# Gate stage of a two-layer hybrid attention network: gate chunks in pairs by seven block products, worked through branch by branch

## Chip, cores and metric

The kernel runs on one core of one Trainium2 chip. The metric is the device time of one launch in microseconds (us). The core's engines are PE (matmul, with a weight-load queue of its own), DVE (vector), ACT (scalar), POOL and SP; SP here only issues DMAs.

## The reference

Input `x` has 512 tokens of width 1024. Two layers; each is a feed-forward part, a token mix, and a second feed-forward part, each with a layer norm. The change lies in the token mix, after its three attentions have made `o_a`, `o_b`, `o_c` (512 tokens x 512 each):

```python
g = jax.nn.sigmoid(h @ w_gate + b_gate).reshape(B, S, N_BRANCH, D)
merged = g[:, :, 0] * (o_a @ w_br_a) + g[:, :, 1] * (o_b @ w_br_b) + g[:, :, 2] * (o_c @ w_br_c)
return merged @ w_out
```

`w_gate` is 1024 x 3072 (three branches of 1024), each `w_br` 512 x 1024, `w_out` 1024 x 1024. All in float32.

## The kernel before

Everything is held transposed: features on the 128 partitions, the 512 tokens along the row. A float32 value is split into a rounded part (`hi`, copied by ACT) and the rest (`lo`, a subtraction on DVE), and a product is three matmuls: hi x hi, hi x lo, lo x hi (`mm3`, lines 182 to 184, in the profile the names `xh`, `xl` for the token side and `hi`, `lo` for the weights). Raw weights come by DMA into a ring of three buffers (`wraw`), and are split into a pair of buffers (`unit`).

A *gate chunk* is 128 of the 3072 gate columns: 8 blocks of 128 rows, so 24 matmuls of 512 columns into one PSUM bank named `gate`, then a tanh on ACT (`gate_ev`, line 1462; the sigmoid is made from it). A *branch chunk* is 128 of 1024 columns of `w_br`: 4 blocks, 12 matmuls into a bank named `brp`. Let (br, d) be chunk d (0 to 7) of branch br (0 to 2). A layer has 24 gate chunks and 24 branch chunks. The gate chunks (0..2, 0) and the matmuls of (0, 1) and (1, 1) are done earlier, as filling between the attention's matmuls (there the bank is called `pj`); the other 19 gate chunks and all branch chunks make up the gate stage.

Before the change the stage goes chunk by chunk: for each d the gates of the three branches, then one item with the branch chunks of branches 1 and 2, and one with that of branch 0. Each item has a load (DMA and split), a matmul part and an evacuation, and loads run three items ahead:

```python
        for i in range(4, len(items)):
            items[i][1]()
            if i + ahead < len(items):
                items[i + ahead][0]()
            items[i][2]()
```

The evacuation multiplies (tanh + 1) with the branch product (line 1593), adds the three branches (1597) and splits the merged chunk into `mh`, `ml` (1599, 1600). The attention outputs of all three branches are split before the stage (1615, 1616). From the fifth item on, PE, POOL, ACT and DVE take their instructions in the written order (`in_order`); SP's order is a scheduler's. After the stage the merged sum is multiplied with `w_out` into eight banks (`acc`, lines 195 to 197), in the same order of four blocks first.

Both feed-forward parts already work in pairs of column chunks by seven block products of 256 columns instead of eight (`strassen`, line 647): four sums of weights (`Pair.sums`, 525 to 528), four sums of tokens made once (`token_sums`), and a few additions on the results (663 to 674). `sums_step` paces, on POOL, a copy of one element and one DMA that prepares weight sums for the next feed-forward part.

Of the kernel before, what the change touches and what calls it, by code (L numbers as in the profile page):

```python
# [13 lines left out]
OP = mybir.AluOpType  # L14
# [50 lines left out]
def body(tc, a, out, depth=DEPTH):  # L65
# [3 lines left out]
    def pool(name, bufs=1, side=None, **kw):  # L69
        return tc.alloc_tile_pool(name=name, bufs=bufs, side=side, **kw)  # L70
# [85 lines left out]
    def wsplit(raw, n=KD, step=None):  # L156
        hi, lo = unit()
        step = step or n
        for i in range(0, n, step):
            c = slice(i, i + step)  # L160
            nc.scalar.activation(hi[:, c], raw[:, c], AF.Copy)  # L161
            nc.vector.tensor_tensor(lo[:, c], raw[:, c], hi[:, c].bitcast(F32), op=OP.subtract)  # L162
# [677 lines left out]
    def mix(l, wts, pend, done_ffn, xap, xa, nxt):  # L840
# [11 lines left out]
        more_close()  # L852

        op = pool("op", side="right", reuse_waits="tile")
        o_t = [[op.tile([P, S], F32, name=f"o{br}{i}") for i in range(4)] for br in range(3)]
# [605 lines left out]
        def gate_ev(t, p, br, d):  # L1461
            nc.scalar.activation(t, p, AF.Tanh, scale=0.5, bias=bg[:, br, d:d + 1])
# [23 lines left out]
        def step(cur, prev, n):  # L1486


            for u in cur:
                while not need(u):  # L1490
                    pump(1)
                    n -= 1
            it, iu = chain(u.tr() for u in prev), chain(u.s() for u in cur)
            nt, ns = sum(u.ngrp for u in prev), sum(u.nseg for u in cur)
            pair = 2
            nt = (nt + pair - 1) // pair
            both = 2 if ns == 2 else 1
# [24 lines left out]
            for _ in it:  # L1522
                pass
            pump(last)
            if prev:
                po = ps("po", "po", (P, 4, P))
                for j, u in enumerate(prev):
                    u.pv(po[:, j])
                while narrow:
                    narrow.popleft()()  # L1530
                for j, u in enumerate(prev):
                    nc.scalar.activation(o_t[u.br][u.m][:, u.qb * P:(u.qb + 1) * P], po[:, j], AF.Copy)
# [8 lines left out]
        at.release()  # L1541
        more_open()
        tp_ = pool("tl", reuse_waits="tile")
        mh = tp_.tile([P, KD, S], F32R, name="mh")
        ml = tp_.tile([P, KD, S], F32R, name="ml")
        ohp = pool("ohp", reuse_waits="tile")
        oh = [[None] * 4 for _ in range(3)]
        ol = [[None] * 4 for _ in range(3)]
        for br in (1, 2, 0):
            for i in range(4):  # L1550
                oh[br][i] = ohp.tile([P, S], F32R, name=f"oh{br}{i}")
                ol[br][i] = ohp.tile([P, S], F32R, name=f"ol{br}{i}")
        def wbr(d, brs):
            r = wraw()
            for j, br in enumerate(brs):
                nc.sync.dma_start(r[:, 4 * j:4 * j + 4],
                                  wb[br].rearrange("(k p) f -> p k f", p=P)[:, :, d * P:(d + 1) * P])
            return wsplit(r[:, 0:4 * len(brs)], 4 * len(brs))

        def gate_item(d, br, bank=None):  # L1560
            st = K()

            def load():
                st.w = wcols(a["w_gate"][l], br * D + d * P)

            def go():
                st.p = ps(bank, "gate")
                proj(st.p, st.w)

            def ev():  # L1570
                t = g_t[d][br] = tp_.tile([P, S], F32, name="t", tag="t", bufs=4)
                gate_ev(t, st.p, br, d)
                sums_step(t)

            return load, go, ev

        def branch_item(d, brs):
            st = K()

            def load():  # L1580
                st.w = wbr(d, brs)

            def go():
                st.p = [ps(name="brp") for _ in brs]
                for j, br in enumerate(brs):
                    for k in range(4):
                        mm3(st.p[j], st.w, 4 * j + k, oh[br][k], ol[br][k], k == 0, k == 3)

            def ev():
                g = g_t[d]  # L1590
                for br, p in zip(brs, st.p):
                    t = g[br]
                    nc.vector.scalar_tensor_tensor(t, t, 1.0, p, op0=OP.add, op1=OP.mult)
                    if br != 2:
                        sums_step(t)
                    if br != 1:
                        nc.vector.tensor_tensor(g[1], g[1], t, op=OP.add)
                if brs[-1] == 0:
                    nc.scalar.activation(mh[:, d], g[1], AF.Copy)
                    nc.vector.tensor_tensor(ml[:, d], g[1], mh[:, d].bitcast(F32), op=OP.subtract)  # L1600

            return load, go, ev

        g_t = [gates0] + [[None] * 3 for _ in range(1, KD)]
        for br in range(2):
            t = g_t[1][br] = tp_.tile([P, S], F32, name="t", tag="t", bufs=4)
            gate_ev(t, held[br], br, 1)
        items = []
        for d in range(KD):
            items += [gate_item(d, br) for br in range(3) if d > 1] + [branch_item(d, brs) for brs in ((1, 2), (0,))]  # L1610
        for f in gate_item(1, 2, "sc"):
            f()
        for br in (1, 2, 0):
            for i in range(4):
                nc.scalar.activation(oh[br][i], o_t[br][i], AF.Copy)
                nc.vector.tensor_tensor(ol[br][i], o_t[br][i], oh[br][i].bitcast(F32), op=OP.subtract)
        ahead = 3
        for i, (load, go, ev) in enumerate(items[:4]):
            load()
            if i == 3:  # L1620
                for load, _, _ in items[4:4 + ahead]:
                    load()
            go()
            ev()
        order = in_order()
# [6 lines left out]
        ohp.release()  # L1632
        op.release()
        xap2, xa2 = alloc_xa()
        ro = pool("ro", side="right", reuse_waits="tile")
# [177 lines left out]
```

## Time and profile before

| | |
|---|---|
| median of 3 runs | 2431.03 us (2430.78 to 2431.32) |
| span of the profiled execution, first to last instruction | 2430.1 us |
| PE busy | 2417.4 us (99%) |
| DVE, ACT, POOL busy | 1837.6, 1192.0, 490.3 us |
| gate stage of layer 0, of layer 1 (us from the span's start) | 667 to 836, 1868 to 2036 |
| granted PE clock | 1.00 throughout |

The profile of one execution gives each engine's instructions with their line, names (written from read), shapes and duration, and the engine or DMA that ended the idle time before them. Matmuls are pipelined: the duration printed of one is longer than the distance to the next, and it is the distance that counts. "x12" marks merged instructions of one kind.

### The profile page before, as it was taken

Reading aid. Unit: us, or ns where it says so; the run is one execution under the profiler, and the core shown is the slowest. Engines: PE = TensorE matmul, PEld = TensorE weight load, DVE = VectorE, ACT = ScalarE, POOL = GpSimd, SP = SyncE. Lnnn points to the kernel's source line nnn. Section 1 sums busy time; section 2 is a strip of 40 time slices with the busy share of each in tenths; the row PEclk is TensorE's granted clock in tenths of the full one; section 3 lists DMA queues with packets and bytes.
Section 4 is the critical chain, followed back from the end, with each engine's and each line's share of the span. In section 5 each row is a group of like instructions: output and inputs, shape, how many; then the busy total and the mean of one; then the engine's idle time right before and its main releaser. Section 6 shows DMA issues by size and latency. Waiting matters only on the chain.

```text
span 2430.1 us, 40766 instructions
## 1 busy us (share of the span) xinstructions
PE 2417.4 (99%) x15448; PEld 2141.6 (88%) x15448; DVE 1837.6 (76%) x3614; ACT 1192.0 (49%) x2304; POOL 490.3 (20%) x684
## 2 busy tenths in 40 slices
PE   9999999999999999999999999999999999999998
PEld 8999887888888899998899998878888888999987
DVE  6899985687654369999879999666776434799997
ACT  4444644577642234445544456455766222344463
POOL 4232402144410001124000004022443100000040
PEclk9999999999999999999999999999999999999999
DMA  7888754676493436887533347546764833333373
GB/s 207 225 224 216 256 159 132 174 166 153 107 254 97 128 105 162 210 209 238 187 109 105 105 129 252 151 139 166 165 141 112 247 104 109 105 99 106 107 241 121
DMA packets 422581, 390.01 MB, mean 160 GB/s; under 512 B 20473, under 2 KB 352393, under 8 KB 422385
## 3 DMA queue, kind: packets, MB, share of 16 engines
q1 hardware_dynamic: 385792, 287.00, 39.8%
q0 software_dynamic: 36592, 100.41, 17.3%
q8 instruction: 122, 2.00, 0.3%
q14 instruction: 75, 0.61, 0.1%
HBM read 360.02 MB, written 93.38 MB: 187 GB/s over the span
## 4 chain that ended last, share of the span: by engine, by line
PE 98%; DMA 1%; issue 0%; ACT 0%; DVE 0%; SPq 0%; DVEq 0%; POOLq 0%; POOL 0%; ACTq 0%
PE acc L331 18%; PE pg L647 17%; PE pu L647 9%; PE pj L182 6%; PE pj L184 6%; PE pj L183 6%; PE pv L647 4%; PE gate L182 3%; PE gate L183 3%; PE gate L184 3%; PE brp L183 2%; PE brp L182 2%; PE brp L184 2%; PE sN L1258 2%; PE ptN L1300 1%; PE po L1319 1%
## 5 line engine op out<-in xcount | busy, mean ns | idle before, releaser
L162 DVE TENSOR_TENSOR lo<-raw,hi 128x1024 fp32r<-128x1024 f32 (+2 forms) x262 | 301.7, 1165 | 248.8 <-ACT hi L161 248.2
L161 ACT ACTIVATE hi<-raw 128x1024 fp32r<-128x1024 f32 (+2 forms) x262 | 258.0, 1003 | 195.2 <-PE acc L331 52.9
L182 PE MATMUL pj<-xh,hi 128*128 128x512 f32 (+1 forms) x720 | 267.0, 371 | 1.0 <-ACT hi L161 1.0
L184 PE MATMUL pj<-xh,lo 128*128 128x512 f32 (+1 forms) x720 | 254.7, 354 | 0.5 <-DVE lo L162 0.5
L183 PE MATMUL pj<-xl,hi 128*128 128x512 f32 (+1 forms) x720 | 254.4, 353 | 0.1
L647 PE MATMUL pg<-xh,lo 128*128 128x256 f32 x864 | 244.5, 283 | 0.0
L647 PE MATMUL pg<-xl,hi 128*128 128x256 f32 x864 | 244.5, 283 | 0.0
L647 PE MATMUL pg<-xh,hi 128*128 128x256 f32 x864 | 244.5, 283 | 0.0
L331 PE MATMUL acc<-hi,sh 128*128 128x512 f32 x568 | 221.5, 390 | 0.0
L331 PE MATMUL acc<-lo,sh 128*128 128x512 f32 x568 | 221.0, 389 | 0.0
L331 PE MATMUL acc<-hi,sl 128*128 128x512 f32 x568 | 221.0, 389 | 0.0
L352 POOL COPY pace<-sh 64x1 f32<-64x1 f32 x16 | 94.5, 5909 | 479.8 <-ACT sh L592 479.8
L544 DVE TENSOR_TENSOR lo<-ws,hi 128x1024 fp32r<-128x1024 f32 x144 | 175.2, 1217 | 0.0
L647 PEld LDWEIGHTS pg<-xl,hi 128*128 128x128 f32 x864 | 165.9, 192 | 0.2
L647 PEld LDWEIGHTS pg<-xh,hi 128*128 128x128 f32 x864 | 165.9, 192 | 0.2
L647 PEld LDWEIGHTS pg<-xh,lo 128*128 128x128 f32 x864 | 165.9, 192 | 0.0
L647 PE MATMUL pu<-th,hi 128*128 128x256 f32 x576 | 163.0, 283 | 0.0
L647 PE MATMUL pu<-tl,hi 128*128 128x256 f32 x576 | 163.0, 283 | 0.0
L647 PE MATMUL pu<-th,lo 128*128 128x256 f32 x576 | 163.0, 283 | 0.0
L184 PEld LDWEIGHTS pj<-xh,lo 128*128 128x128 f32 x720 | 136.1, 189 | 20.4 <-DVE lo L162 0.8
L541 ACT ACTIVATE hi<-ws 128x1024 fp32r<-128x1024 f32 x144 | 143.9, 1048 | 16.9 <-DVE ws L526 15.3
L182 PEld LDWEIGHTS pj<-xh,hi 128*128 128x128 f32 x720 | 136.4, 189 | 16.7 <-issue 3.7
(374 smaller groups left out, 6645.9 us busy)
## 6 DMA issues: line engine op xcount, KB each, us to landing
raw<-in_ffn_w_dram SPq DMA_DIRECT2D x228, 512.0 KB, 4.5
ts<-in_ffn_w_dram POOLq DMA_DIRECT2D x72, 768.0 KB, 7.5
raw<-in_w_in_dram SPq DMA_DIRECT2D x56, 512.0 KB, 4.1
raw<-ts SPq DMA_DIRECT2D x52, 512.0 KB, 4.2
raw<-in_w_gate_dram SPq DMA_DIRECT2D x48, 512.0 KB, 4.1
ts<-ts POOLq DMA_DIRECT2D x24, 768.0 KB, 8.7
x_sp<-xa POOLq DMA_DIRECT2D x24, 512.0 KB, 6.3
ks<-hl SPq DMA_DIRECT2D x96, 128.0 KB, 2.4
```

Of the source, the lines that this page charges most:

```text
L161: nc.scalar.activation(hi[:, c], raw[:, c], AF.Copy)
L162: nc.vector.tensor_tensor(lo[:, c], raw[:, c], hi[:, c].bitcast(F32), op=OP.subtract)
L182: nc.tensor.matmul(o, hi[:, k], vh, start=first, stop=False)
L183: nc.tensor.matmul(o, hi[:, k], vl, start=False, stop=False)
L184: nc.tensor.matmul(o, lo[:, k], vh, start=False, stop=last)
L331: nc.tensor.matmul(o, xx[:, t], ww[:, c], start=first and i == 0, stop=last and i == 2)
L352: nc.gpsimd.tensor_copy(pace[0:64], sp(min(p + 1, NS - 1))[0][0:64, 0, 0:1].bitcast(F32))
L541: nc.scalar.activation(t[0], x, AF.Copy)
L544: nc.vector.tensor_tensor(t[1], x, t[0].bitcast(F32), op=OP.subtract)
L647: nc.tensor.matmul(o, wx, vx, start=first and k == 0 and i == 0, stop=k == 3 and i == 2, skip_group_check=True)
L1258: nc.tensor.matmul(o[:, 0:nb].rearrange("p k b j -> p (k b j)"), q, kx[:, 2 * b0:2 * (b0 + nb)].rearrange("p a b -> p (a b)"), start=i == ...
L1300: nc.tensor.transpose(pt[:, k, br], p[:, k, br], ident)
```

## The change

The gate stage is rewritten. It goes branch by branch: 1, then 2, then 0, each with one merged sum `acc` in SBUF that collects the products. The attention output of a branch is split only when its turn comes, into one buffer `ob` for all three branches (`split_o`). Fourteen of the 24 gate chunks of a layer are done in seven pairs: (1, 6..7), and (2, 2..7), (0, 2..7). The five others of the stage stay as they were. A branch's weights are loaded and split for two chunks at a time (`branch_w`).

The four token sums of the pairs are made at the stage's start on DVE and ACT, in the place `mm` where `mh` and `ml` go at the end. The 12 steps for that are put between the plain chunks (`some(2)`). A pair (`Two`) has four sums of weights on DVE, three full splits and one of half size; `cycle` runs one pair on PE, makes the next pair's sums and splits in between, and then runs one or two pairs of branch chunks. In the cycles of (2, 2) and (0, 2) there are two pairs of branch chunks; the second's weights are split inside the loop, into the buffer of an attention output that is no longer needed. The core of the diff:

```diff
-        for i in range(4, len(items)):
-            items[i][1]()
-            if i + ahead < len(items):
-                items[i + ahead][0]()
-            items[i][2]()
...
+        def split_o(br, n=2):
+            for k in range(0, 4, n):
+                c = slice(k, k + n)
+                parts(ob[0][:, c], ob[1][:, c], o_t[br][:, c])
...
+            def sums(u):
+                rg, ru = u.rg, u.ru
+                u.ws = op.tile([P, 2, KD, P], F32, name="ws", tag="o1")
+                u.x1, u.x2 = x1, x2 = u.ws[:, 0], u.ws[:, 1]
+                tt(x1[:, lo4], ru[:, lo4], ru[:, hi4], op=OP.add)
+                tt(x1[:, hi4], x1[:, lo4], rg[:, lo4], op=OP.subtract)
+                tt(x2[:, lo4], rg[:, lo4], ru[:, lo4], op=OP.subtract)
+                tt(x2[:, hi4], rg[:, hi4], x1[:, hi4], op=OP.subtract)
...
+        def branch(br, d, w, mid=None):
+            for j in range(2):
+                p = ps(name="brp")
+                for k in range(4):
+                    mm3(p, w, 4 * j + k, ob[0][:, k], ob[1][:, k], k == 0, k == 3)
+                if mid and j == 0:
+                    mid()
+                t, o = g[br, d + j], acc[:, d + j]
+                if br == 1:
+                    stt(o, t, 1.0, p, op0=OP.add, op1=OP.mult)
+                else:
+                    stt(t, t, 1.0, p, op0=OP.add, op1=OP.mult)
+                    tt(o, o, t, op=OP.add)
+            tick(o)
...
+        def cycle(cur, nxt, brps, end=None):
+            ga, pa, pb = (ps(name="gate") for _ in range(3))
+            if nxt:
+                nxt.sums()
+            br, d = brps[0]
+            w = branch_w(br, d, wt)
+            prod(ga[:, H1], cur.ug, 0, XP)
+            prod(ga[:, H2], cur.u1, 0, T[0], False)
+            sn, v, h = temp("sn"), temp("v"), gate_t(cur.br, cur.d + 1)
+            nc.scalar.activation(sn, ga, AF.Copy)
+            if nxt:
+                nxt.hi("ug")
+            prod(pa[:, H1], cur.u1, 4, T[1])
+            prod(pa[:, H2], cur.u2, 0, T[2], False)
+            tt(v[:, H1], pa[:, H1], sn[:, H1], op=OP.add)
+            tt(v[:, H2], pa[:, H2], v[:, H1], op=OP.add)
+            tt(h[:, H2], sn[:, H2], v[:, H2], op=OP.add)
+            if nxt:
+                nxt.hi("u1")
+            prod(pb[:, H1], cur.ud, 0, T[3])
+            tt(h[:, H1], pb[:, H1], v[:, H2], op=OP.add)
+            prod(ga[:, H1], cur.ug, 4, XR, False)
+            prod(ga[:, H2], cur.u2, 4, XS, False)
+            if nxt:
+                nxt.hi("ud")
+            t = gate_t(cur.br, cur.d)
+            nc.scalar.activation(h, h, AF.Tanh, scale=0.5, bias=bg[:, cur.br, cur.d + 1:cur.d + 2])
+            tt(ga[:, H2], ga[:, H2], v[:, H1], op=OP.add)
+            gate_ev(t, ga, cur.br, cur.d)
+            tick(t)
+            mid = (lambda: nxt.hi("u2")) if nxt else end
+            for i, (br, d) in enumerate(brps):
+                branch(br, d, w if i == 0 else branch_w(br, d, op), mid)
+                mid = None
...
+        plain(1, 4, wp[5])
+        some(2)
+        plain(1, 5, wp[6])
+        some(2)
+        cur.sums()
+        cur.hi("ug")
+        branch(1, 4, wp[7])
+        for n in ("u1", "u2", "ud"):
+            cur.hi(n)
+        todo = deque([(2, 2), (2, 4), (2, 6), (0, 2), (0, 4), (0, 6)])
+        then = Two(*todo.popleft())
+        brps = {(1, 6): [(1, 6)], (2, 2): [(2, 0), (2, 2)], (0, 2): [(0, 0), (0, 2)]}
...
+        while cur:
+            me = cur.br, cur.d
+            if me[1] == 2:
+                split_o(me[0])
+            cycle(cur, then, brps.get(me, [me]), merged)
+            cur, then = then, Two(*todo.popleft()) if todo else None
+        for d in (6, 7):
+            parts(mh[:, d], ml[:, d], acc[:, d])
```

Here `parts(hi, lo, x)` is a copy on ACT and a subtraction on DVE, `prod` is 12 matmuls of 256 columns (four blocks, three each), `plain` one gate chunk the old way, and `merged`, the `end` of the last cycle, splits the merged sum's chunks 0 to 5.

Two places show the new order. The first is DVE's queue. Before, in the middle of the stage of layer 0 (chunk 3: `brp_8264`, `brp_8265` are the branch chunks of branches 1 and 2, `brp_8299` that of branch 0, `lo` the low halves of weights of later items):

```order
L162 TENSOR_TENSOR lo_8259<-raw_8256,hi_8258 128x1024
L162 TENSOR_TENSOR lo_8293<-raw_8290,hi_8292 128x1024
L1593 SCALAR_TENSOR_TENSOR t_8229<-t_8229,brp_8264 128x512
L1593 SCALAR_TENSOR_TENSOR t_8262<-t_8262,brp_8265 128x512
L1597 TENSOR_TENSOR t_8229<-t_8229,t_8262 128x512
L162 TENSOR_TENSOR lo_8315<-raw_8312,hi_8314 128x1024
L1593 SCALAR_TENSOR_TENSOR t_8196<-t_8196,brp_8299 128x512
```

Now, at the end of the cycle of (2, 2) (`lo_8411` is the last low half of the next pair; `brp_8397` and `brp_8416` are the first pair of branch chunks, `brp_8437` and `brp_8452` the second; `wo_8434` holds the second pair's weights, high and low, and this row writes the low half):

```order
L1709 TENSOR_TENSOR gate_8276<-gate_8276,v_8316 128x256
L1560 TENSOR_TENSOR lo_8411<-ws_8279,hi_8410 128x1024
L1675 SCALAR_TENSOR_TENSOR g02_4277<-g02_4277,brp_8397 128x512
L1676 TENSOR_TENSOR acc_7761<-acc_7761,g02_4277 128x512
L1675 SCALAR_TENSOR_TENSOR g12_7768<-g12_7768,brp_8416 128x512
L1676 TENSOR_TENSOR acc_7761<-acc_7761,g12_7768 128x512
L1560 TENSOR_TENSOR wo_8434<-raw_8431,wo_8434 128x1024
L1675 SCALAR_TENSOR_TENSOR t_8393<-t_8393,brp_8437 128x512
```

The low half of weights used to stand items ahead of the products that need it; the one of the second pair now stands behind both products of the first pair and directly ahead of its own.

The second is ACT's queue. Before, in the stage of layer 0 (tanh of chunk 2's gates, between them high halves of later weights):

```order
L1462 ACTIVATE t_8036<-gate_8004,bgate_82 128x512
L161 ACTIVATE hi_8067<-raw_8065 128x512
L1462 ACTIVATE t_8071<-gate_8040,bgate_82 128x512
L161 ACTIVATE hi_8100<-raw_8098 128x1024
L1462 ACTIVATE t_8104<-gate_8073,bgate_82 128x512
L161 ACTIVATE hi_8134<-raw_8132 128x1024
```

Now, at the last two plain chunks (`t_8021` is the tanh of (1, 4), `t_8056` that of (1, 5); `mm_7757<-x_7797` are the high halves of token sums, `hi_8069`, `hi_8101`, `hi_8105` and `dh_7764` those of the first pair's weights and weight sums):

```order
L1462 ACTIVATE t_8021<-gate_7996,bgate_82 128x512
L1559 ACTIVATE mm_7757<-x_7797 128x512 x2
L1462 ACTIVATE t_8056<-gate_8031,bgate_82 128x512
L1559 ACTIVATE mm_7757<-x_7797 128x512 x2
L1559 ACTIVATE hi_8069<-raw_7992 128x1024
L1559 ACTIVATE hi_8101<-ws_8064 128x1024
```

The last two token sums' copies now stand behind the tanh of the last plain chunk, and the first pair's weights behind them.

More of the change, by code (lines that the diff above doesn't have):

```diff
@@ L854, in mix @@
         op = pool("op", side="right", reuse_waits="tile")
-        o_t = [[op.tile([P, S], F32, name=f"o{br}{i}") for i in range(4)] for br in range(3)]
+        o_t = [op.tile([P, 4, S], F32, name=f"o{br}", tag=f"o{br}") for br in range(3)]
         at = pool("at", reuse_waits="tile")
@@ L1543, in mix @@
         tp_ = pool("tl", reuse_waits="tile")
[L1544 to L1553, printed above, removed]
-            r = wraw()
[L1555 to L1625, printed above, removed]
-        for i in range(4, len(items)):
-            items[i][1]()
-            if i + ahead < len(items):
-                items[i + ahead][0]()
-            items[i][2]()
+        mm = tp_.tile([P, 2, KD, S], F32R, name="mm")
+        mh, ml = mm[:, 0], mm[:, 1]
@@ new lines, in mix @@
+        gp = pool("gp", reuse_waits="tile")
+        acc = gp.tile([P, KD, S], F32, name="acc")
+        ob = [gp.tile([P, 4, S], F32R, name=n) for n in ("oh", "ol")]
+        gd = [gp.tile([P, 4, P], F32R, name=n) for n in ("dh", "dl")]
+        g1 = [gp.tile([P, S], F32, name=f"g1{br}") for br in range(3)]
+        gw = a["w_gate"][l]
+        tt, stt = nc.vector.tensor_tensor, nc.vector.scalar_tensor_tensor
+        lo4, hi4, H1, H2 = slice(0, 4), slice(4, 8), slice(0, 256), slice(256, 512)
@@ new lines, in mix, with parts, pair_of @@
+        for br in range(2):
+            gate_ev(g1[br], held[br], br, 1)
+        order = in_order()
+        def parts(hi, lo, x):
+            nc.scalar.activation(hi, x, AF.Copy)
+            tt(lo, x, hi.bitcast(F32), op=OP.subtract)
+        def split_o(br, n=2):
+            for k in range(0, 4, n):
+                c = slice(k, k + n)
+                parts(ob[0][:, c], ob[1][:, c], o_t[br][:, c])
+        def pair_of(pl):
+            return [pl.tile([P, KD, P], F32R, name=n, tag=n, bufs=3 if pl is wt else 2) for n in ("hi", "lo")]
@@ new lines, in raw_of, with gate_w, branch_w @@
+        def raw_of(w, c0, ks=range(KD)):
+            r = wraw()
+            n = len(ks)
+            nc.sync.dma_start(r[:, 0:n], w.rearrange("(k p) f -> p k f", p=P)[:, :, c0:c0 + P])
+            return r
+        def gate_w(br, d, pl):
+            r = raw_of(gw, br * D + d * P)
+            u = pair_of(pl)
+            parts(*u, r)
+            return u
+        def branch_w(br, d, pl):
+            r = wraw()
+            v = wb[br].rearrange("(k p) f -> p k f", p=P)
+            for j in range(2):
+                nc.sync.dma_start(r[:, 4 * j:4 * j + 4], v[:, :, (d + j) * P:(d + j + 1) * P])
+            if pl is op:
+                u = op.tile([P, 2, KD, P], F32R, name="wo", tag="o2")
+                u = u[:, 0], u[:, 1]
+            else:
+                u = pair_of(pl)
+            parts(*u, r)
+            return u
@@ new lines, in tick, with token_sums, back, both @@
+        def tick(t):
+            sums_step(t[:, 0:1] if len(t.shape) == 2 else t[:, 0, 0:1])
+        th, tl = (t.rearrange("p a (b s) -> p (a b) s", s=256) for t in (mh, ml))
+        T = [(th[:, 4 * i:4 * i + 4], tl[:, 4 * i:4 * i + 4]) for i in range(4)]
+        XP, XR, XS = [(xh[:, k, c], xl[:, k, c]) for k, c in ((lo4, H1), (hi4, H1), (hi4, H2))]
+        def token_sums(g):
+            x = op.tile([P, 4, S], F32, name="x", tag="o1")
+            steps = []
+            def back(i):
+                c, o = slice(4 * i + 2 * g, 4 * i + 2 * g + 2), slice(2 * i, 2 * i + 2)
+                tt(x[:, o], xh[:, c].bitcast(F32), xl[:, c].bitcast(F32), op=OP.add)
+            p_, q, r_, s_ = x[:, 0:2, H1], x[:, 0:2, H2], x[:, 2:4, H1], x[:, 2:4, H2]
+            def both(i, o, u, v):
+                tt(o, u, v, op=OP.subtract)
+                c = slice(2 * g, 2 * g + 2)
+                parts(T[i][0][:, c], T[i][1][:, c], o)
+            steps += [lambda i=i: back(i) for i in range(2)]
+            for z in ((0, p_, q, p_), (2, q, s_, q), (1, s_, s_, p_), (3, r_, r_, s_)):
+                steps.append(lambda z=z: both(*z))
+            return steps
@@ new lines, in mix, with __init__, hi @@
+        class Two:
+            def __init__(u, br, d):
+                u.br, u.d = br, d
+                u.rg, u.ru = raw_of(gw, br * D + d * P), raw_of(gw, br * D + (d + 1) * P)
+            def sums(u):
[6 more added lines that the diff above has]
+                tt(x2[:, hi4], rg[:, hi4], x1[:, hi4], op=OP.subtract)
+            def hi(u, n):
+                x = {"ug": u.rg, "u1": u.x1, "u2": u.x2, "ud": u.ru[:, hi4]}[n] if n != "ug" else u.rg
+                t = gd if n == "ud" else pair_of(more.pool if n == "ug" else wt)
+                setattr(u, n, t)
+                parts(*t, x)
@@ new lines, in prod @@
+        def prod(o, w, k0, x, first=True):
+            for k in range(4):
+                hi, lo = w[0][:, k0 + k], w[1][:, k0 + k]
+                vh, vl = x[0][:, k], x[1][:, k]
+                for i, (wx, vx) in enumerate(((hi, vh), (hi, vl), (lo, vh))):
+                    nc.tensor.matmul(o, wx, vx, start=first and k == 0 and i == 0, stop=k == 3 and i == 2,
+                                     skip_group_check=True)
+        g = {(br, d): t for d, ts_ in ((0, gates0), (1, g1)) for br, t in enumerate(ts_)}
@@ new lines, in gate_t, with plain @@
+        def gate_t(br, d):
+            g[br, d] = t = gp.tile([P, S], F32, name="t", tag="t", bufs=4)
+            return t
+        def plain(br, d, w, t=None):
+            p = ps(name="gate")
+            proj(p, w)
+            t = gate_t(br, d) if t is None else t
+            gate_ev(t, p, br, d)
+            tick(t)
+        def branch(br, d, w, mid=None):
+            for j in range(2):
+                p = ps(name="brp")
+                for k in range(4):
+                    mm3(p, w, 4 * j + k, ob[0][:, k], ob[1][:, k], k == 0, k == 3)
[4 more added lines that the diff above has]
+                    stt(o, t, 1.0, p, op0=OP.add, op1=OP.mult)
+                else:
+                    stt(t, t, 1.0, p, op0=OP.add, op1=OP.mult)
+                    tt(o, o, t, op=OP.add)
+            tick(o)
@@ new lines, in temp @@
+        def temp(n):
+            return gp.tile([P, S], F32, name=n, tag=n, bufs=2)
+        def cycle(cur, nxt, brps, end=None):
[27 more added lines that the diff above has]
+            gate_ev(t, ga, cur.br, cur.d)
+            tick(t)
+            mid = (lambda: nxt.hi("u2")) if nxt else end
+            for i, (br, d) in enumerate(brps):
+                branch(br, d, w if i == 0 else branch_w(br, d, op), mid)
+                mid = None
@@ new lines, in mix, with some @@
+        wp = [gate_w(2, 1, wt)]
+        split_o(1)
+        wp.append(branch_w(1, 0, more.pool))
+        wp.append(gate_w(1, 2, wt))
+        steps = [f for i in range(2) for f in token_sums(i)]
+        def some(n):
+            for _ in range(n):
+                steps.pop(0)()
+        plain(2, 1, wp[0], g1[2])
+        wp.append(gate_w(1, 3, wt))
+        some(2)
+        branch(1, 0, wp[1])
+        wp.append(branch_w(1, 2, more.pool))
+        plain(1, 2, wp[2])
+        some(2)
+        wp.append(gate_w(1, 4, wt))
@@ new lines, in mix @@
+        plain(1, 3, wp[3])
+        some(2)
+        wp.append(gate_w(1, 5, wt))
+        branch(1, 2, wp[4])
+        some(2)
+        wp.append(branch_w(1, 4, more.pool))
+        cur = Two(1, 6)
+        plain(1, 4, wp[5])
+        some(2)
+        plain(1, 5, wp[6])
+        some(2)
+        cur.sums()
[5 more added lines that the diff above has]
+        then = Two(*todo.popleft())
@@ new lines, in mix, with merged @@
+        brps = {(1, 6): [(1, 6)], (2, 2): [(2, 0), (2, 2)], (0, 2): [(0, 0), (0, 2)]}
+        def merged():
+            for d in range(0, 6, 2):
+                c = slice(d, d + 2)
+                parts(mh[:, c], ml[:, c], acc[:, c])
+        while cur:
[6 more added lines that the diff above has]
+            parts(mh[:, d], ml[:, d], acc[:, d])
@@ L1631, in mix @@
         order.__exit__(None, None, None)
-        ohp.release()
+        gp.release()
         op.release()
```

2 lines of the change are left out of this document (1 added, 1 removed).

## The prediction

> **What bounds the kernel now.** I read the page's head, then the chain of work that ended last, then who waited for whom on PE.
>
> ```profile
> span 2430.1 us, 40766 instructions
> PE 98%; DMA 1%; issue 0%; ACT 0%; DVE 0%; SPq 0%; DVEq 0%; POOLq 0%; POOL 0%; ACTq 0%
> ```
> ```profile
> PE hid L1030 <- DMA cw<-in_cmp_k_w_dram: 1.7, 2, 1.3
> PE warm L1659 <- DVE xl L1656: 1.5, 1, 1.5
> PE pj L182 <- ACT hi L161: 1.0, 1, 1.0
> PE pj L184 <- DVE lo L162: 0.5, 1, 0.5
> ```
> The chain is PE for 98% of the span, and PE waits 4.7 us in all, nowhere in the gate stage. So a matmul cycle saved there is time saved, and every wait put on PE there is time lost. Two stretches by window, the gate stage of layer 0 and the loop of the first feed-forward part that already works by seven block products:
>
> ```profile
> 667.00:836.00 169.00, 169.00 (x752) 139.82 (x748) 76.59 (x93) 56.93 (x78) 9.34 (x12) 1.00 0.57 161
> 67.00:229.00 162.00, 162.00 (x1353) 162.00 (x1352) 149.80 (x227) 74.73 (x97) 47.96 (x71) 1.00 0.88 229
> ```
> Columns after the window: busy PE, PE weight loads, DVE, ACT, POOL, then clock, DMA share, GB/s. In the gate stage DVE works 77 of 169 us; in the loop 150 of 162, and PE still has no gap. DVE's room is thus not the question; its order is.
>
> **What is removed.** Matmuls of 512 columns are read from the timeline, twelve apart; those of 256 from the chain of the loop:
>
> ```profile
> 672.88 0.39 PE L182 MATMUL brp<-oh,hi 128*128 128x512 f32 x1
> 675.60 0.39 PE L182 MATMUL brp<-oh,hi 128*128 128x512 f32 x1
> ```
> ```profile
> 106.62 1.44 PE pv L647 x12
> 108.06 5.76 PE pg L647 x48
> 113.82 2.88 PE pu L647 x24
> ```
> 2.72 us for 12 is 0.2267 us each; 5.76 us for 48 is 0.120 us each, a little over half. Two gate chunks the old way are 48 x 0.2267 = 10.88 us; as a pair 7 products x 12 x 0.120 = 10.08 us (5.76 + 2.88 + 1.44, as in the chain). That saves 0.80 us a pair and, for 7 pairs in each of 2 layers, **11.2 us**. The branch matmuls (288 a layer) and the ten plain gate chunks stay as they are. Nothing else leaves PE.
>
> **What is added, and the walk along the queues.** DVE and ACT now take the whole stage in the written order. Their rates, from the timeline of the same loop:
>
> ```profile
> 151.10 0.28 PE L647 MATMUL pg<-xh,hi 128*128 128x256 f32 x1
> ```
> ```profile
> 151.30 0.43 DVE L674 TENSOR_TENSOR pg<-pg,v 128x256 f32<-128x256 f32 x1 [0.37 <-PE pg L647]
> 153.01 0.68 DVE L525 TENSOR_TENSOR ws<-raw 128x512 f32<-128x512 f32 x1
> 153.72 0.69 DVE L526 TENSOR_TENSOR ws<-ws,raw 128x512 f32<-128x512 f32 x1
> 154.33 0.68 DVE L527 TENSOR_TENSOR ws<-raw 128x512 f32<-128x512 f32 x1
> 157.06 0.42 DVE L663 TENSOR_TENSOR v<-pu,sn 128x256 f32<-128x256 f32 x1
> 157.52 0.42 DVE L664 TENSOR_TENSOR v<-pu,v 128x256 f32<-128x256 f32 x1
> 158.32 1.22 DVE L544 TENSOR_TENSOR lo<-ws,hi 128x1024 fp32r<-128x1024 f32 x1
> 159.45 0.42 DVE L668 TENSOR_TENSOR ha<-pv,v 128x256 f32<-128x256 f32 x1
> ```
> ```profile
> 154.18 0.60 ACT L657 ACTIVATE sn<-pg 128x512 f32<-128x512 f32 x1 [1.81 <-PE pg L647]
> 155.62 1.99 ACT L541 ACTIVATE hi<-ws 128x1024 fp32r<-128x1024 f32 x2
> ```
> ```profile
> L1462 ACT ACTIVATE t<-gate,bgate 128x512 f32<-128x512 f32 x38 | 26.1, 686 | 94.3 <-PE gate L184 94.3
> L1593 DVE SCALAR_TENSOR_TENSOR t<-t,brp 128x512 f32<-128x512 f32 x42 | 28.7, 684 | 23.3 <-PE brp L184 23.1
> ```
> ```profile
> raw<-in_w_gate_dram SPq DMA_DIRECT2D x48, 512.0 KB, 4.1
> ```
> From start to start, DVE takes 1.14 us for a low half of 1024, 0.61 for 512 (0.71 if the next reads its result) and 0.34 for 256 (0.46); a lone low half lasts 1.22. ACT takes 0.95 for a high half of 1024 (lasts 1.05), 0.63 for 512, 0.69 for a tanh. The DVE addition starts 0.20 us after PE's last matmul of the block was followed by the next (151.10 to 151.30); I take 0.2 for the way back to PE as well, an estimate from that row.
>
> *A plain pair cycle* is 10.08 + 24 x 0.2267 = 15.52 us of PE. DVE's list (four sums, four low halves of 1024, one of 512, five additions of 256, two products, two additions) comes to about 12.3 us by these rates, ACT's to about 6. Laid out in order, the low half of the next pair's third sum ends 13.6 us into the cycle and is read 4.3 us into the next; the branch weights' low half ends at 5.2 and is read at 10.1. Cost 0: PE's own 15.52 us covers it, as in the loop.
>
> *The two cycles with two branch pairs a layer* (those of the chunks 2 and 3 of the third and of the first branch) are another matter. The second pair's weights are split on DVE after both product-and-add couples of the first pair, and the second couple waits for the first pair's last matmul. Call that moment X. With DVE idle: product at X+0.20, addition 0.71 later, low half 0.61 later, which ends at X+2.74; PE goes on at X+2.95, but had matmuls without that low half only up to X+0.45. Floor: 2.5 us of wait. DVE is not idle. At the cycle's start stand the splits of the next attention output (2 x 1.14, from 1.5 us), then the sums; so the list is late: third sum's low half at 14.25, products and additions from 15.4, low half 18.0 to 19.25, PE on at 19.3 in place of 15.97: **3.3 us**. That is the cycle of the first branch. The cycle of the third branch starts with DVE 2 us later still, because in the cycle before it the raw weights arrive late: three raw buffers are left, the second half of the pair is fetched only when DVE is done with the first pair's buffer, and with 4.1 us a fetch the branch weights land 10.8 us into that cycle. ACT's copy of the first products is queued behind their high half and ends at 12.4, the high half that DVE needs next at 13.4, and DVE's last product ends 3.65 us into the next cycle. From there the same list (two splits to 5.9, sums to 8.5, low halves, additions, third sum's low half to 17.4, couples from 17.3, low half 19.9 to 21.15) gives PE on at 21.35: **5.4 us**.
>
> *Entry to the first pair.* ACT's last two token-sum copies stand behind the tanh of the last plain chunk, which ends on PE at Y. Tanh Y+0.2, copy to Y+1.43, low half, difference, copy, low half to Y+4.1, four weight sums to Y+6.7, low half of the first pair to Y+7.8. PE has only one branch pair (5.44 us) meanwhile and needs the low half at Y+5.68, gets it at Y+8.0: 2.35 us; the next operand's low half comes two products later at Y+10.2, 0.95 us more. **3.3 us**.
>
> *Start of the stage.* Old rows:
>
> ```profile
> 667.29 0.50 PE L182 MATMUL gate<-xh,hi 128*128 128x512 f32 x1
> ```
> ```profile
> 667.43 0.45 ACT L1532 ACTIVATE o<-po 128x128 f32<-128x128 f32 x2 [2.58 <-PE po L1319]
> 667.76 1.27 ACT L1462 ACTIVATE t<-pj,bgate 128x512 f32<-128x512 f32 x2
> 668.90 6.37 ACT L1615 ACTIVATE oh<-o 128x512 fp32r<-128x512 f32 x12
> ```
> Now only one branch's output is split there, but the first branch weights come after it: ACT 668.90 + 0.95 + 0.95 + 1.05, DVE's low half to 673.5; PE wants it at 672.88 + 0.45. **0.2 us**.
>
> *End of the stage.* Four splits of output weights, the last tanh and three splits of the merged sum stand before the last product-and-add couples, whose banks the seventh and eighth accumulator want 19.6 and 20.3 us into the last cycle; the second product ends at 20.95. About 1 us, and the loads of the four residual rows, which now stand on SP's queue just ahead of these output weights and can't go before the last sums' buffer is read, may hold them up: I take **1.2 us**, bounds 0 and 2.5.
>
> Sum a layer: 0.2 + 3.3 + 5.4 + 3.3 + 1.2 = 13.4 us of PE waits against 5.6 saved. Two layers: +26.8 - 11.2 = **+15.6 us**, from the profiled 2430.1 to 2445.7. The median of the runs is 0.9 above that span, so 2446.6. Costed at nothing: POOL's six pacing copies and DMAs now come 5 us apart and end before a gate buffer is reused; SP's DMAs, as many bytes as before, on queues whose share in this stage is 0.57 (the window's row).
>
> [...] PE's clock after a wait is seen only at the start of this trace:
>
> ```profile
> 1.52 3.17 PE L1659 MATMUL warm<-xl 128*128 128x512 bf16 x7 [1.52 <-DVE xl L1656]
> ```
> Seven matmuls of 512 columns in 3.17 us, 0.45 each, twice the 0.2267 of later. If a wait of 5.4 us brings that back, seven at 0.45 for 0.2267 lose 1.6 us a time. [...]
>
> **Rivals.**
> 1. The waits come near their floors: 2 x 2.5 + 2.3 = 7.3 us a layer, 14.6 - 11.2 = +3.4: 2434.4. For it: DVE has 12.3 of 15.5 us to do and could catch up. Against: the order holds the late list in front of the split.
> 2. My waits, and the clock falls in both 5.4 us waits: 2446.6 + 3.2 = 2449.8.
> 3. Faster: PE never waits, 2431.0 - 11.2 = 2419.8. This is the loop's case, the same cycle of 10.08 us on a fuller DVE. It decides below 5.6 us of waits a layer; the two floors of 2.5 us alone are 5.0, so every other wait would have to go.
>
> **How the numbers follow.** 0.2% (4.9 us) is about what a measurement of this kernel tells from no change. My waits 0.67, rival 2 0.17, rival 1 0.12, rival 3 0.04. The forecast is the first: 2446.6. Low: waits of 0, 2.3, 3.3, 3.3, 0 a layer, 17.8 - 11.2: 2437.6. High: 0.5, 4.3, 6.5, 4.0, 2.5, 35.6 - 11.2: 2455.4, which takes in rival 2. Below and above lie 0.16 and 0.04. Slower by over 0.2% takes the first two and part of rival 1: 0.85; the rest of it 0.11; faster 0.04.
>
> **What would show it.** Right: 84 matmuls of 256 columns at 0.120 us a pair; in the list of PE's waits, `brp` on DVE `wo` twice a layer at 3 to 6 us, `gate` on DVE `lo` at 2 to 3 us once a layer, and none in the cycles with one branch pair. Wrong: no PE wait over 1 us in the stage, plain cycles longer than 15.6 us (then DVE or the raw buffers bound them all), or a `brp` wait on DMA.

## The result, and the profile after

The changed kernel took 2452.25 us (median; 2451.67 to 2453.74), the one before 2431.00 beside it: a ratio of 1.0088, 95% interval 1.0075 to 1.0100. It is slower by 21 us; the forecast was 2446.6 with a range to 2455.4. The profiled execution is the slowest of its five (2453.74). The head of the page, the chain of work that ended last, and PE's waits after the change:

```profile
span 2452.0 us, 41947 instructions
PE 93%; DVE 4%; issue 1%; ACT 1%; DMA 1%; SPq 0%; DVEq 0%; POOLq 0%; ACTq 0%; POOL 0%
```
```profile
PE brp L184 <- DVE wo L1560: 12.0, 4, 3.0
PE gate L1648 <- DVE lo L1560: 4.9, 3, 2.1
PE gate L1648 <- ACT sn L1691: 1.8, 2, 1.3
PE pg L182 <- ACT ha L586: 1.1, 2, 0.6
PE acc L195 <- DVE t L1675: 0.7, 2, 0.4
```

DVE holds 4% of the chain where it held none, and PE's list of waits has five new rows in the stage and just behind it. The first two were forecast by name and the last (`acc`, the end of the stage) by its place; the third (`sn`) and the fourth (`ha`, in the feed-forward part after the stage) were not. A plain pair cycle takes what was forecast: its first matmul stands at 757.47 and that of the next cycle at 773.02, 15.55 us against 15.52.

```profile
757.47 0.28 PE L1648 MATMUL gate<-xh,hi 128*128 128x256 f32 x1
773.02 0.28 PE L1648 MATMUL gate<-xh,hi 128*128 128x256 f32 x1
```

What PE loses is read from start to start: the distance of two matmuls less what one takes in a full stream (0.2267 us for 512 columns, 0.120 for 256). By that, the two layers lose, in us:

| place | forecast | layer 0 | layer 1 |
|---|---|---|---|
| start of the stage | 0.2 | 0.30 | 0.30 |
| entry to the first pair | 3.3 | 3.3 | 3.1 |
| wait for `sn`, cycle (1,6) | 0 | 1.5 | 0.8 |
| wait for `wo`, cycle (2,2) | 5.4 | 3.2 | 3.2 |
| wait for `wo`, cycle (0,2) | 3.3 | 3.1 | 3.2 |
| end of the stage | 1.2 | 1.0 | 1.0 |
| wait for `ha` in the part after | 0 | 0.8 | 0.8 |
| matmuls at half clock behind waits | 0 | 3.4 | 2.7 |
| sum | 13.4 | 16.6 | 15.1 |

31.7 us lost less 11.2 saved is 20.5 of the 21.9 by which the two profiled spans differ; the other 1.4 us lie outside the two stages, spread over the span, and were not taken apart.

The half clock is the row that the forecast put at nothing. Windows by stretch (busy PE, weight loads, DVE, ACT, POOL, then granted clock, DMA share, GB/s), ahead of a `wo` wait, behind three of them, behind an entry wait, and behind the fourth `wo` wait:

```profile
740.00:747.00 7.00, 7.00 (x39) 6.05 (x38) 5.16 (x10) 3.31 (x4) 0.00 (x0) 1.00 0.80 227
750.60:754.40 3.80, 3.72 (x9) 2.95 (x10) 0.03 (x1) 0.13 (x1) 0.00 (x0) 0.55 0.46 138
808.90:812.40 3.50, 3.50 (x10) 2.71 (x10) 1.05 (x2) 0.00 (x0) 0.00 (x0) 0.51 0.50 145
1968.20:1973.00 4.80, 4.73 (x14) 3.73 (x15) 1.03 (x3) 1.03 (x1) 0.00 (x0) 0.64 0.38 109
1931.00:1935.00 4.00, 3.82 (x19) 3.54 (x20) 4.00 (x6) 0.66 (x2) 0.00 (x0) 0.62 0.46 131
2025.20:2029.00 3.80, 3.75 (x16) 3.06 (x17) 1.07 (x2) 0.17 (x1) 0.00 (x0) 1.00 0.46 138
```

One of these stretches matmul by matmul, from PE's timeline:

```profile
807.68 0.50 PE L184 MATMUL brp<-oh,wo 128*128 128x512 f32 x1 [2.95 <-DVE wo L1560]
808.01 0.40 PE L182 MATMUL brp<-oh,wo 128*128 128x512 f32 x1
808.95 0.62 PE L183 MATMUL brp<-ol,wo 128*128 128x512 f32 x1
809.36 0.63 PE L184 MATMUL brp<-oh,wo 128*128 128x512 f32 x1
...
811.92 0.60 PE L184 MATMUL brp<-oh,wo 128*128 128x512 f32 x1
812.35 0.41 PE L182 MATMUL brp<-oh,wo 128*128 128x512 f32 x1
812.59 0.40 PE L183 MATMUL brp<-ol,wo 128*128 128x512 f32 x1
```

PE comes back from the wait at 807.68 and runs at full rate for 1.3 us. At 808.95 the distance goes from 0.23 to 0.43 us, for 3.4 us, and then back.

### The profile page after: what moved, and what is told of

Its sections match the earlier page's. It is cut to its first block, busy times and chain, and to the rows that moved or that the text cites. A ratio compares the mean times of both kernels' runs of the same rounds, so it can differ in the third digit from the quotient of the medians.

```text
span 2452.0 us, 41947 instructions
## 1 busy us (share of the span) xinstructions
PE 2418.8 (99%) x15952; PEld 2160.7 (88%) x15952; DVE 1947.3 (79%) x3782; ACT 1229.1 (50%) x2336; POOL 487.8 (20%) x684
## 4 chain that ended last, share of the span: by engine, by line
PE 93%; DVE 4%; issue 1%; ACT 1%; DMA 1%; SPq 0%; DVEq 0%; POOLq 0%; ACTq 0%; POOL 0%
PE acc L331 17%; PE pg L647 17%; PE pu L647 8%; PE pj L182 6%; PE pj L183 6%; PE pj L184 6%; PE pv L647 4%; PE gate L1648 3%; PE sN L1258 2%; PE ptN L1300 1%; PE po L1319 1%; PE brp L184 1%; PE acc L195 1%; PE brp L183 1%; PE brp L182 1%; PE acc L197 1%
## 5 line engine op out<-in xcount | busy, mean ns | idle before, releaser
L162 DVE TENSOR_TENSOR lo<-raw,hi 128x1024 fp32r<-128x1024 f32 (+2 forms) x192 | 223.8, 1183 | 95.9 <-ACT hi L161 95.2
L161 ACT ACTIVATE hi<-raw 128x1024 fp32r<-128x1024 f32 (+2 forms) x192 | 192.1, 1020 | 130.0 <-PE acc L331 54.6
```

## The experiments

My theory after the result was that the whole difference is waits and the half clock that they set off, each wait with its own place in DVE's or ACT's written order. All kernels are edits of the changed one; ratios are to the kernel before.

**The second branch pair's split ahead of the first pair's products.**

```diff
-                branch(br, d, w if i == 0 else branch_w(br, d, op), mid)
+            ws2 = [w] + [branch_w(*x, op) for x in brps[1:]]
+            for w, (br, d) in zip(ws2, brps):
+                branch(br, d, w, mid)
```

> The second branch pair's weights are split on ScalarE and VectorE before the first branch pair's products instead of behind them; the arithmetic is the same. Theory A (waits, and the half clock after them): the four waits of brp on wo (3.21, 3.12, 3.21, 3.12 = 12.7 us) go, and with them the half-clock stretches behind three of them (1.69 + 1.56 + 1.5 us); the changed kernel's 2452.3 comes to about 2435, at most 1 us more where VectorE's list in the cycle of chunk 2 of the third branch is still late. Rival B (the clock falls for a reason of its own, not for the wait): the waits go and the slow stretches stay, 2439.5. Rival C (the split pushes VectorE's products back, and the wait comes back as a wait for a bank or for the next pair's low half): 2440 to 2446, with new PE waits of 1 us and more in the next cycle.

Measured 2435.48 us, ratio 1.0018 (1.0009 to 1.0027): 16.8 us back, as theory A says. The rows of `brp` on `wo` are gone from PE's waits, nothing took their place there, and where the waits were the clock is whole. Behind the two entry waits it is not; the last two rows are those places:

```profile
PE gate L1648 <- DVE lo L1560: 4.3, 2, 2.1
PE gate L1648 <- ACT sn L1691: 1.1, 2, 0.6
```
```profile
745.00:751.00 6.00, 6.00 (x27) 4.88 (x26) 5.26 (x7) 1.94 (x3) 0.00 (x0) 1.00 0.59 172
800.00:806.00 6.00, 6.00 (x31) 5.03 (x30) 4.89 (x9) 1.06 (x1) 0.00 (x0) 1.00 0.32 90
714.00:717.40 3.40, 3.40 (x18) 3.40 (x18) 3.40 (x5) 0.21 (x1) 0.00 (x0) 0.50 0.53 154
1922.30:1925.70 3.40, 3.40 (x17) 3.30 (x17) 3.40 (x5) 0.00 (x0) 0.00 (x0) 0.50 0.53 154
```

So the place of one split is four fifths of the loss. B and C fall: no slow stretch stays behind the branch products, and no wait comes back. The two that stay stand behind the waits of 2.3 us at the entries, one more than in the changed kernel.

**The same split between the two couples of the first pair.**

```diff
+                if between and j == 0:
+                    between()
...
+                more_w = (lambda: ws2.append(branch_w(*brps[1], op))) if i == 0 and len(brps) > 1 else None
+                branch(br, d, ws2[i], mid, more_w)
```

> The same split stands between the first and the second product-and-addition couple, so that one couple (0.71 + 0.61 us from start to start) comes off the way to it; the arithmetic is the same. Theory A: each of the four waits shortens from 3.2 to about 1.9 us (5 us in all), and waits of 1.9 us trip the clock seldom: the 2.3 us wait at the entry did so in one layer of two. With none tripped 2452.3 - 5 - 4.8 = 2442.5, with half of them 2445. Rival B (the clock falls for a reason of its own): the slow stretches stay, 2447.3.

Measured 2443.65 us, ratio 1.0051 (1.0039 to 1.0064); theory A had 2442.5 with no fall of the clock. The four waits are 1.8 to 1.9 us from start to start, and none sets off the half clock, nor does any other wait in the two stages:

```profile
PE brp L184 <- DVE wo L1560: 6.7, 4, 1.7
```
```profile
749.90:753.90 4.00, 4.00 (x18) 3.23 (x19) 2.53 (x4) 0.38 (x1) 0.00 (x0) 1.00 0.44 131
```

**TensorE kept busy through the wait.** Twelve more matmuls whose sums are cleared by the ones that follow; the order on the other engines is untouched.

```diff
+                for _ in range(fill if j == 0 else 0):
+                    nc.tensor.matmul(p, w[0][:, 0], ob[0][:, 0], start=True, stop=True)
...
+                branch(br, d, w if i == 0 else branch_w(br, d, op), mid, 12 * i)
```

> Twelve more matmuls of 512 columns (2.72 us) stand ahead of the second branch pair's products in the two long cycles of each layer, into the bank that these products then clear; they fill TensorE's wait, and the order on the other engines is the same. Theory A (idle time trips the clock): TensorE is busy through what was a wait, what is left of it is 0.4 us, and the half-clock stretches behind the branch waits go: 2452.3 - 4.8 = 2447.5 with 48 more matmuls. Rival B (clock falls for a reason of its own): 2452.3, with the slow stretches there. Rival D (the added matmuls are not hidden): 2452.3 + up to 10.9.

Measured 2447.88 us, ratio 1.0069 (1.0056 to 1.0081): 4.4 us less with 48 matmuls more, at the number of theory A. The waits shrink to 0.3 and 0.4 us, and behind them the clock stays whole (one stretch of half clock is left in the stages, behind an entry wait):

```profile
PE brp L184 <- DVE wo L1560: 0.5, 2, 0.2
```
```profile
751.00:755.00 4.00, 4.00 (x17) 3.27 (x18) 1.34 (x2) 0.18 (x1) 0.00 (x0) 1.00 0.44 131
```

This is the run that shows the cause: the same matmuls at the same place with the same operands run at full rate when PE was not idle before them.

**The wait as long as the longer one was forecast.**

```diff
+            for _ in range(2 if pl is op else 0):
+                tt(u[1], r, u[0].bitcast(F32), op=OP.subtract)
```

> The second branch pair's low half is computed three times over (the same values), which puts 2.28 us more between the first pair's products and the second pair: each of the four waits on wo then lasts about 5.4 us, as long as the longer of them was forecast. Theory A (a longer wait only makes the fall of the clock surer, its price stays 1.6 us): 2452.3 + 9.1 + 1.6 for the one wait of four that did not trip = 2463. Rival H (the price grows with the wait): 2466 and more. Rival I (the fall has to do with what comes after the wait, and stays at three of four): 2461.4.

Measured 2466.97 us, ratio 1.0147 (1.0132 to 1.0163). The four waits are 5.6 to 5.7 us from start to start, each sets off the half clock, and behind them 1.6, 2.6, 2.6 and 1.5 us more are lost, 2.1 on average against 1.7 behind the waits of 3.2. That is nearer rival H than A, whose fixed price was too low. The price does not grow smoothly: three of the four stretches of half clock last 6.83 us here and one 3.41, where all four of the changed kernel's last 3.41; the last section says when.

```profile
PE brp L184 <- DVE wo L1594: 22.0, 4, 5.6
```
```profile
752.90:758.00 5.10, 4.96 (x15) 3.96 (x16) 0.92 (x3) 1.06 (x1) 0.00 (x0) 0.67 0.34 103
812.30:818.30 6.00, 5.84 (x15) 4.60 (x16) 1.24 (x3) 0.70 (x1) 0.00 (x0) 0.55 0.32 90
```

**The copy `sn` ahead of the branch weights' high half.**

```diff
-            br, d = brps[0]
-            w = branch_w(br, d, wt)
...
             nc.scalar.activation(sn, ga, AF.Copy)
+            br, d = brps[0]
+            w = branch_w(br, d, wt)
```

> ScalarE's copy of the first products stands ahead of the branch weights' high half, which waits for a late DMA; the arithmetic is the same. Theory A: the waits of gate on sn (1.43 us in layer 0, 0.69 in layer 1) go, but VectorE's list loses the same time of catching up, and the next cycle's wait of brp on wo grows from 3.2 to 4.6 and 3.9 us: 2452.3, within 0.7. Rival E (the sn wait is time of its own): 2450.2, with the wo waits at 3.2.

Measured 2452.91 us (2450.91 to 2454.60), ratio 1.0088 (1.0074 to 1.0102): the time of theory A, but not by its way. The `sn` waits are gone from the list. The waits on `wo` in (2,2) grew by 0.33 and 0.28 us, not by 1.4 and 0.7. What filled the gap is the half clock, which falls at other places than before: more behind the entry (0.7 us) and both (0,2) waits (1.1 and 1.6), less behind one in (2,2), a wait of 3.5 us with no fall at all (the second window):

```profile
PE brp L184 <- DVE wo L1560: 12.6, 4, 3.4
```
```profile
807.10:813.00 5.90, 5.90 (x14) 4.64 (x15) 1.22 (x2) 0.00 (x0) 0.00 (x0) 0.51 0.33 92
1968.20:1973.00 4.80, 4.80 (x21) 3.88 (x22) 1.38 (x2) 0.00 (x0) 0.00 (x0) 1.00 0.36 109
```

Neither theory is shown by the total; the length of a wait alone does not decide the fall. More on that in the last section.

**The entry in another order.**

```diff
-        some(2)
-        plain(1, 5, wp[6])
-        some(2)
+        some(4)
         cur.sums()
         cur.hi("ug")
+        plain(1, 5, wp[6])
+        cur.hi("u1")
         branch(1, 4, wp[7])
...
```

> At the entry to the first pair the last token sums, the first pair's weight sums and its first two weight splits stand ahead of the last plain chunks' evaluations instead of behind them; the arithmetic is the same. Theory A: the two entry waits of a layer and the half clock behind them go (2.41 + 0.90 us in layer 0, 4.06 in layer 1, 7.4 in all); the branch weights' transfer, which waits for a buffer, doesn't come as much earlier as TensorE does, so the wait for sn grows by about 1 us in each layer: 2452.3 - 7.4 + 2 = 2447, and 2445 where it doesn't grow. Rival F (the transfer sets the time of that cycle, not the entry): the sn wait takes back all that the entry gives, 2451 to 2452.

Measured 2449.78 us (2447.78 to 2456.78), ratio 1.0081 (1.0068 to 1.0093), between the two. The five times spread over 9 us, so 2.5 us less than the changed kernel is not clear of noise; what holds is read from the trace, of an execution of 2452.18. The entry waits fall to 0.95 us a layer, but the `sn` waits grow to 2.4 and 2.3 (from start to start), and the second sets off 1.5 us of half clock. That the branch weights' transfer sets these waits, as F has it, is an estimate from the changed kernel, where ACT is idle for 7.31 us ahead of their high half (its row at 721.43, below).

```profile
PE gate L1648 <- ACT sn L1691: 4.3, 2, 2.2
PE gate L1648 <- DVE lo L1560: 1.4, 2, 0.7
```

**The three edits together** (early split, `sn` first, entry).

> The three edits together: the second branch pair's split early, the copy sn ahead of the branch weights, the entry in the new order; the arithmetic is the same. Theory A (the waits add up, and no other stands behind them): the 2435.5 of the early split less 7.8 us for the entries with their half clock and 1.5 for sn is 2426, below the kernel before by 5; what is left beside the 11.2 us saved are about 2 us a layer at the start and the end of the stage and in the next stage. Rival F (VectorE's list or the late transfer shows up as a new wait in the first pair cycle): 2428 to 2431.

Measured 2431.12 us, ratio 1.0000 (0.9991 to 1.0009). Theory A is wrong by 5 us and the time is rival F's: the waits do not simply add up. The new wait is not where F had it, though (the first pair's cycle), but one cycle on. The entry keeps 0.95 us a layer, and the long cycle of chunk 2 of the third branch has a new wait, first for ACT's high half and then for DVE's low half of the same weights, 1.7 and 1.6 us in all. PE's waits, and ACT's timeline there:

```profile
PE gate L1648 <- DVE lo L1560: 1.4, 2, 0.7
PE brp L182 <- ACT wo L1559: 1.2, 2, 0.7
PE brp L184 <- DVE wo L1560: 1.1, 2, 0.5
```
```profile
741.25 0.72 ACT L1708 ACTIVATE t<-t,bgate 128x512 f32<-128x512 f32 x1 [4.67 <-DVE t L1702]
742.13 0.69 ACT L1462 ACTIVATE t<-gate,bgate 128x512 f32<-128x512 f32 x1 [0.16 <-DVE gate L1709]
742.71 1.05 ACT L1559 ACTIVATE wo<-raw 128x1024 fp32r<-128x1024 f32 x1
```

ACT was idle for 4.67 us ahead of the two tanh and the split stood behind them: a place in the order, not a rate.

**The new order without the pairs** (all chunks plain, no token sums).

> The branch-by-branch order with its merged banks and wide splits, but all chunks plain: no token sums and no pairs, so 48 matmuls of 512 columns for two chunks. Theory A (the order costs nothing but the small waits at the start and the end of the stage and in the next, 0.3 + 1.0 + 0.8 us a layer, all else is the pairs' list): 2431.0 + 4.2 = 2435, some 9 to 11 us above the three edits together. Rival G (the order itself puts TensorE in wait, by fewer raw buffers): 2440 and more, with waits of brp or gate inside the stage.

Measured 2433.51 us, ratio 1.0009 (1.0001 to 1.0018): the order branch by branch by itself costs 2.4 us, little over half of what A allowed for, and G falls. PE waits for no `brp` or `gate` operand in the stage; its chain is the old one:

```profile
PE 98%; DMA 1%; issue 0%; ACT 0%; DVE 0%; DVEq 0%; POOLq 0%; SPq 0%; POOL 0%; ACTq 0%
```

All but 2.4 us of the loss thus comes with the pairs and their list, the late split among it: this kernel also loads and splits every branch's weights three items ahead, so it does not tell the two apart. Against it the three edits with pairs are 2.4 us faster, not 11.2: some 10 us of waits remained in the stages of that kernel and just behind them.

**Three more moves.** On top of the three: the second split ahead of the tanh, the token sums three at a time so that they are done a chunk earlier, the merged sum's first splits ahead of the last tanh.

```diff
+            else:
+                end()
+            ws2 = [w] + [branch_w(*x, op) for x in brps[1:]]
             t = gate_t(cur.br, cur.d)
             nc.scalar.activation(h, h, AF.Tanh, scale=0.5, bias=bg[:, cur.br, cur.d + 1:cur.d + 2])
...
-        some(2)
+        some(3)
```

> The three edits and three more: the second branch pair's split stands ahead of the tanh (the high half waited 0.7 us behind two tanh of ScalarE), the token sums go three at a time so that they are done before the chunk ahead of the entry, and the merged sum's first three splits stand ahead of the last tanh; the arithmetic is the same. Theory A (each wait left in the stage is a place in a list): the 2431.1 of the three edits less 3.3 us (the long cycle of chunk 2 of the third branch, 1.73 + 1.58), 1.9 (entry, 0.94 + 0.95) and 2 of the 2.4 at the end is 2424, below the kernel before by 7. Rival K (a split put ahead only pushes what stood there behind, and the time is lost in the next cycle): 2428 to 2431.

Measured 2426.05 us (2424.08 to 2428.32), ratio 0.9978 (0.9969 to 0.9987), between A and K: faster than both kernels by 4.9 and 26 us. The rows for the entry's `gate` on `lo` and for the end's `acc` are gone from PE's list. What is left inside the stage is 0.6 us a layer for `brp` on `lo`, and in the second layer alone 1.7 us in the long cycle. The profiled execution is the slowest of the eleven, with one stretch of half clock outside the stages, behind a wait for a transfer:

```profile
PE pg L182 <- ACT ha L586: 1.1, 2, 0.6
PE brp L184 <- DVE lo L1560: 0.6, 2, 0.4
PE brp L182 <- ACT wo L1559: 0.6, 1, 0.6
PE brp L184 <- DVE wo L1560: 0.5, 1, 0.5
```

## Why the prediction came out as it did

**Direction, and the saving: right.** Pair cycles cost 15.55 us of PE, so 11.2 us are saved; PE pays more than that in waits, at the places named, for the reason named (the split stands behind both couples). The run with the early split gives those waits back.

**Start, entry, (0,2), end: right.** 0.2, 3.3, 3.3 and 1.2 us were forecast; 0.3, 3.1 to 3.3, 3.1 to 3.2 and 1.0 were measured. The floor of 2.5 us below each `wo` wait held: with the split at its place and PE not filled, the shortest `wo` wait of any run is 2.47 us, in the run with the other entry.

**The wait in (2,2): 5.4 us forecast, 3.2 measured.** The step that failed is DVE's lateness at that cycle's start. I put DVE's last product 3.65 us into the cycle; it ends 1.63 into it. The rows: PE's wait in the cycle before, ACT's two steps, DVE's last product there, the first matmul of (2,2), the end of its wait, and the split that ends it:

```profile
723.03 0.39 PE L1648 MATMUL gate<-xh,hi 128*128 128x256 f32 x1 [1.27 <-ACT sn L1691]
```
```profile
721.43 1.06 ACT L1559 ACTIVATE hi<-raw 128x1024 fp32r<-128x1024 f32 x1 [7.31 <-DMA raw<-in_w_br_b_dram]
722.40 0.58 ACT L1691 ACTIVATE sn<-gate 128x512 f32<-128x512 f32 x1
```
```profile
731.82 1.28 DVE L1673 SCALAR_TENSOR_TENSOR acc<-t,brp 128x512 f32<-128x512 f32 x2
```
```profile
731.47 0.28 PE L1648 MATMUL gate<-xh,hi 128*128 128x256 f32 x1
750.68 0.62 PE L184 MATMUL brp<-oh,wo 128*128 128x512 f32 x1 [3.04 <-DVE wo L1560]
```
```profile
749.41 1.22 DVE L1560 TENSOR_TENSOR wo<-raw,wo 128x1024 fp32r<-128x1024 f32 x1
```

I had the late transfer right (10.8 us into the cycle; ACT starts on it at 721.43, 10.3 after the cycle's first matmul at 711.11), and saw that `sn` is queued behind it. But I followed only DVE from there. PE itself needs the copy: the second products of the first bank are accumulated into a bank that ACT has still to read. So PE lost 1.5 us in that cycle and the next one began as much later; DVE itself came 0.5 us sooner than forecast, as the transfer did. Together that is the 2.0 us by which DVE was less late. From there the walk held: from DVE's last product to the end of the split 17.5 us were forecast (3.65 to 21.15), and 17.5 passed (733.10 to 750.63). The run with `sn` first bears this out: there DVE's last product ends 2.2 us into (2,2), with no wait for `sn` ahead of it, and the wait for `wo` is 3.5 us. A walk must put down each wait on PE's own line before it carries the others on.

**The clock: rival 2 named the fall, and counted too few.** It had the clock fall behind the two waits of 5.4 us and behind none of the shorter ones; no run shows such a limit between 3.3 and 5.4 us. There was no wait of 5.4, and of the four of 3.1 to 3.2 us three tripped it, and of two entry waits of 2.3 us one did; 6.1 us in all, where rival 2 had 3.2. This is nearly the whole difference between the forecast and the result (5.7 us): the errors on (2,2) (-4.4), `sn` (+2.3) and `ha` (+1.6) nearly cancel. That the time lies in the range is partly luck: with waits of 5.4 us in (2,2) and all else as measured it would have been 2456.7, outside it.

**Not foreseen and not settled:** 0.8 us a layer in the feed-forward part after the stage (`pg` on `ha`), which stands at that place in every kernel with pairs, not in the one without, and was not taken apart. POOL's pacing copies, costed at nothing, show in no wait of PE's in the stage; SP's transfers show only through the late branch weights ahead of `sn`.

## What to carry to other kernels

When a saving on the bounding engine is paid for with more steps on engines in written order, walk the order with absolute times for every engine at once, the bounding engine's own small waits included; a step that needs only its operands, put behind one that waits for the bounding engine, cost that engine a stop all four times here. Allow for more than the stop itself: in the gate stages here the clock fell behind stops of 2.3 to 5.7 us, though not behind every one, and behind none of the four of 1.8 to 1.9 us; when it fell, the stop cost another 0.6 to 1.0 us at the entry (where a second, shorter wait went in part into the slow stretch) and 1.5 to 2.6 us at the split. Moving such steps ahead one at a time shows the next wait behind the last, so expect less than the sum.

## What the runs showed of the hardware

In the gate stages of these runs PE's clock fell to half at the end of an interval, on a grid fitted to its changes, in which PE was idle for about 2 us; the length of the wait alone does not tell. The traces hold each change of the granted clock. In the changed kernel it is 0.50 in four stretches of 3.413 us, which end at 754.33, 812.36, 1935.35 and 1972.89 us, 17.0, 329.0 and 11.0 times that length apart. In the run with waits of 5.7 us the half-clock stretches end at 756.28, 817.73, 1940.71, 1981.67 and 2039.70 us, which are 18.0, 329.0, 12.0 and 17.0 times 3.413 us apart; each lasts one interval of that length or two (3.41 or 6.83 us). From these lengths and distances I took a grid of 3.413 us, laid it through the changes of each run and added up, for each interval in the gate stages of the eleven kernels, the time that PE lost in it from start to start. The clock fell 21 times, each time behind an interval with 2.02 us or more; of the intervals that it did not fall behind, the most idle have 2.03 and 1.99. Some of them, by the wait that fills them:

| run | wait, us | length | idle in one interval | clock falls |
|---|---|---|---|---|
| entry | 1964.2 to 1966.7 | 2.5 | 1.37 | no |
| changed kernel | 2022.1 to 2025.3 | 3.1 | 1.97 | no |
| `sn` first | 1964.6 to 1968.1 | 3.5 | 1.98 | no |
| changed kernel | 711.3 to 713.6 | 2.3 | 2.03 | no |
| entry | 2019.0 to 2022.1 | 3.1 | 2.02 | yes |
| `sn` first | 804.0 to 807.1 | 3.1 | 2.13 | yes |
| changed kernel | 804.6 to 807.7 | 3.1 | 2.25 | yes |
| entry | 1936.0 to 1938.3 | 2.3 | 2.26 | yes |
| changed kernel | 1928.9 to 1931.2 | 2.3 | 2.40 | yes |
| changed kernel | 747.5 to 750.7 | 3.2 | 3.19 | yes |

The bound was fitted afterwards and the idle time is a difference of starts, so 2.0 is good to perhaps 0.1 us. It says why one wait of 3.5 us was free and one of 2.3 cost extra, and why the four of 1.8 to 1.9 us never did (they are shorter than the bound). A slow interval was followed by a second one where 1.1 us or more of it was idle (five times), and by the full clock where 0.7 or less was (21 times); that is what the longest waits paid for. The grid does not lie at one place of the span: that of the run with waits of 5.7 us stands 1.95 us behind that of the changed kernel (756.28 against 754.33). Whether this is why executions of one kernel differ by some us is not shown, with one profiled execution of each. One fall does not fit as it stands: outside the stages, in the last run, at 1621.69 us, behind a wait of 1.85 us (1.6 in PE's list of waits) of which 1.63 lie in one interval; the matmuls around it are of other shapes, whose streaming times I did not work out.
